# Operands of matrix products moved to addresses that are multiples of 512 bytes, in a four-layer trunk on one Trainium2 core

## The chip, the cores and the metric

The kernel runs on one core of one Trainium2 chip. The metric is the device time of one execution in microseconds (us). A core has a matrix engine (TensorE, called PE in the profile, with its weight loads shown apart as PEld), a vector engine (VectorE, DVE), an activation engine (ScalarE, ACT), GpSimd (POOL), and queues that start transfers (SP, ACT and POOL). Its working memory has 128 partitions; an address here is a byte offset inside a partition, and all 128 partitions use the same one.

## The reference

The model takes 512 tokens of 1,024 features through four sublayers, each added to the residual stream after a root-mean-square norm: multi-head latent attention (MLA), a feed-forward layer (MLP), gated linear attention (GLA), and a second MLP; a last norm follows.

```python
for i in range(DEPTH):                    # DEPTH = 2
    xn = rms_norm(x, norm_mix[i])
    mix = mla_mixer(xn, ...) if i % 2 == 0 else gla_mixer(xn, ...)
    x = x + mix
    x = x + jnp.square(jax.nn.relu(rms_norm(x, norm_mlp[i]) @ w_up[i])) @ w_down[i]
return rms_norm(x, final_norm)
```

MLA has 8 heads, projections of low rank for queries (384) and for keys and values (256), a rotary key and a causal softmax over 512 keys. GLA has 4 heads with a decay per key feature, accumulated over the sequence. The MLPs go from 1,024 to 4,096 features and back.

## The kernel before

Everything is float32. A product is made of three passes on the matrix engine: each operand is split into a high part (the rounded copy, type fp32r) and a low part (the rest), and high x high, high x low and low x high are summed (`mm3`, lines 109 to 114). In a pass the *stationary* operand, 128 columns (512 bytes of a partition), is loaded into the array, and the *moving* operand, up to 512 columns (2,048 bytes), streams past it. A pass on a type other than fp32r is issued twice by the compiler, except transposes (`tr`, line 129), which multiply by the tile `ident`.

Weights come from memory into the tiles `wraw` and `comb`, are split by ACT (line 104) and DVE (line 107) into `wh` and `wl`, and are used at once. Activations live in tiles called `set`, 2,048 or 4,096 bytes each. Each MLP works by blocks of 512 hidden features with a seven-product scheme on quarters of the matrices: `up_product` (line 939) has moving operands of 256 columns, which are either parts of the `set` tiles ("11", "21", "22") or of four combined tiles `T1` to `T4` (the profile calls them `T`, since it leaves numbers out); `down_product` (line 948) has moving operands of 512 columns out of `wh` and `wl` and stationary ones out of `set`.

The order of the instructions on each engine comes from a scheduler and a few explicit rules of order in the kernel. Tiles are placed by pools: `const` and `sb` live to the end, `rk` (`rope_keep`), `keep` and `pp` (attention), `ap` (`mla_attn`), `fast` (MLP) and `gp` (GLA) live for a stage and share the room above. A pool's tiles follow each other, each rounded up to 32 bytes; small tiles between large ones shift all that follow. A tile with one value or a few per partition (`stat`, `srstd`, `cols`, `gms`, `D`, `rtok`) costs 32 bytes.

In the built program before, 265 tiles `wh`, 265 `wl` and all 158 `set` tiles begin 32 bytes past a multiple of 512; `T1` to `T4` and `comb` 320 past; the latent tiles of attention `cq..` 128 past, and `ckv..`, `kh`, `kl`, `qh`, `ql`, `KA`, `KB`, `PTh` and `PTl` 192 past; GLA's `ADh` and `qd` 320 past, its `kth`, `ktl` and `S` 384 past; `ident` 128 past.

Of the passes on fp32r, by columns of the moving operand and by whether both operands stand at the same offset past a multiple of 512 (counted in the built program):

| columns | same offset before | other offsets before | same offset after | other offsets after |
|---|---|---|---|---|
| 512 | 2,744 | 212 | 2,934 | 22 |
| 384 | 24 | 40 | 64 | 0 |
| 256 | 1,032 | 1,504 (of these `T`: 1,344) | 2,536 | 0 |
| 128 | 0 | 16 | 16 | 0 |

Of the kernel before, what the change touches and what calls it, by code (L numbers as in the profile page):

```python
# [18 lines left out]
P = 128  # L19
D = 1024  # L20
# [30 lines left out]
def trunk_kernel(ctx: ExitStack, tc: tile.TileContext, t_in: dict, out: bass.AP):  # L51
# [71 lines left out]
            return ACT.activation(*a, **k)  # L123

    ident = const.tile([P, P], F32, name="ident")
    make_identity(nc, ident)

    def tr(psum, src):
# [18 lines left out]
    rope_es = ExitStack()  # L147
    rk = rope_es.enter_context(tc.tile_pool(name="rope_keep", bufs=1, reuse_waits="tile"))

    gains = const.tile([P, N_GAIN + NT + 32], F32, name="gains")  # L150
    pos_i = gains[:, N_GAIN : N_GAIN + NT].bitcast(I32)
    invf = gains[:, N_GAIN + NT :]

# [5 lines left out]
    def load_x(q, j):  # L159
        q.dma_start(xall[:, j], x_in[:, j])  # L160

    eps_t = const.tile([P, 1], F32, name="eps_t")
    DVE.memset(eps_t, EPS)
    one_t = const.tile([P, 1], F32, name="one_t")
    DVE.memset(one_t, 1.0)
    ones_r = const.tile([P, P], F32R, name="ones128")
    ones128 = f(ones_r)
    DVE.memset(ones128, 1.0)
    ident_b = rk.tile([P, P], BF16, name="ident_b")
# [2 lines left out]
    DVE.memset(causal, 0.0)  # L172
    POOL.affine_select(causal, causal, [[-1, P]], ALU.is_ge, NEG, base=0, channel_multiplier=1)

    def inv_tile(n, pool):
        t = pool.tile([P, P], F32R, name=f"inv{n}")
        DVE.memset(f(t), 1.0 / n)
        return t

    inv_dr = inv_tile(D, const)  # L180
    inv_d = f(inv_dr)

    RB = 32
    row_eps = rk.tile([3 * RB, 1], F32, name="row_eps")
    row_mix = rk.tile([3 * RB, 1], F32, name="row_mix")
    for r, (e, m) in enumerate(((EPS * EPS, EPS), (Q_PART * EPS * EPS, Q_PART * EPS), (EPS, 1.0))):
        DVE.memset(row_eps[r * RB : (r + 1) * RB], e)
        DVE.memset(row_mix[r * RB : (r + 1) * RB], m)  # L190
# [82 lines left out]
    def small_rstd(ms, n, scale):  # L273
        l = sm(n)
        act_e(l, ms, AF.Ln, bias=eps_t, scale=scale)
        y0 = sm(n)
        act_e(y0, l, AF.Exp, scale=-0.5)
        e = sm(n)
        DVE.tensor_scalar(e, ms, scale, EPS, ALU.mult, ALU.add)
        a = sm(n)  # L280
        DVE.tensor_tensor(a, e, y0, ALU.mult)
        b = sm(n)
        DVE.scalar_tensor_tensor(b, a, -0.5, y0, ALU.mult, ALU.mult)
        r = sb.tile([P, n], F32, tag="srstd", bufs=4, name=uname("srstd"))
        DVE.scalar_tensor_tensor(r, b, 1.5, y0, ALU.add, ALU.mult)
        return r

# [5 lines left out]
    def rope_turns():  # L293
        sh = (P, NT, 32)
        es = ExitStack()
        rp = es.enter_context(tc.tile_pool(name="rope", bufs=1, reuse_waits="tile"))

        def tmp(shape, dt=F32):
            return rp.tile(list(shape), dt, tag="rope", bufs=8, name=uname("rope"))

        pos = tmp((P, NT))
        POOL.tensor_copy(pos, pos_i)
        ang, part = tmp(sh), tmp(sh)
        POOL.tensor_tensor(
            ang, pos.unsqueeze(2).to_broadcast([P, NT, 32]), invf.unsqueeze(1).to_broadcast([P, NT, 32]), ALU.mult
        )
        ah = tmp(sh, F32R)
        POOL.tensor_copy(ah, ang)
        al = tmp(sh)
        POOL.tensor_tensor(al, ang, f(ah), ALU.subtract)  # L310
        frac = Fraction("0.15915494309189533576888376337251436203445964574046")
        c = []
        for _ in range(4):
            e = 0
            while frac * 2**e < 2048:
                e += 1
            c.append(Fraction(int(frac * 2**e), 2**e))
            frac -= c[-1]
        c = [float(v) for v in c]

        def wrap(t):
            m = part
            POOL.tensor_scalar(m, t, 1.0, MAGIC, ALU.mult, ALU.add)
            POOL.tensor_scalar(m, m, 1.0, -MAGIC, ALU.mult, ALU.add)
            POOL.tensor_tensor(t, t, m, ALU.subtract)

        acc = tmp(sh)
        POOL.tensor_scalar(acc, f(ah), c[0], 0.0, ALU.mult, ALU.add)
        wrap(acc)
        wrap(acc)  # L330
        for src, n, wraps in ((f(ah), 1, 1), (al, 0, 1), (f(ah), 2, 1), (al, 1, 1), (f(ah), 3, 0), (al, 2, 0), (al, 3, 0)):
            t = tmp(sh)
            POOL.tensor_scalar(t, src, c[n], 0.0, ALU.mult, ALU.add)
            for _ in range(wraps):
                wrap(t)
            POOL.tensor_tensor(acc, acc, t, ALU.add)
        r = rk.tile([P, 2, NT, 32], F32, name="rope_turns")
        for n, shift in enumerate((0.25, 0.0)):
            t = tmp(sh)
            POOL.tensor_scalar(t, acc, 1.0, shift, ALU.mult, ALU.add)  # L340
            wrap(t)
            POOL.tensor_scalar(r[:, n], t, 0.4999999, -0.4999999, ALU.min, ALU.max)
        es.close()
        return r
# [29 lines left out]
    def mla(layer, nrm, first, pools):  # L374
# [111 lines left out]
        for t in range(NT):  # L486
            tk = slice(t * P, (t + 1) * P)
            for hf in range(2):
                p = bank("bc"[hf])
                for k in range(2):  # L490
                    mm3(p, cut(CVL[k], slice(None), tk), cut(wv[k], slice(None), 0, slice(hf * 512, hf * 512 + 512)), k == 0, k == 1)
                if (t, hf) == (1, 1):
                    pr = bank("c")
                    for i in range(NT):
                        tr(pr[:, i * 3 * RB : (i + 1) * 3 * RB], rows[:, i * P : (i + 1) * P])
                    cols = keep.tile([P, NT, 3], F32, tag="cols", name="cols")
                    DVE.tensor_copy(cols, pr[:, : NT * 3 * RB].rearrange("p (t a r) -> p t a r", t=NT, a=3)[:, :, :, 0])
                    VP.append((1, 1, p))
                    for i in (1, 0, 3, 2):
                        evac_v(*VP[i])  # L500
                elif t < 2:
                    VP.append((t, hf, p))
                else:
                    evac_v(t, hf, p)
            if t == 1:
                r_kv = sb.tile([P, S], F32, tag="rstd", bufs=2, name=uname("rstd"))
                for i in range(P // RB):
                    SP.dma_start(r_kv[i * RB : (i + 1) * RB], rows[:RB])
                for j in range(2):
                    y = tmp()  # L510
                    DVE.scalar_tensor_tensor(y, pkv[j], gcol("kvn", 2 * layer + j), r_kv, ALU.mult, ALU.mult)
                    hi, lo = (keep.tile([P, S], F32R, tag=f"ckv{j}{x}", name=f"ckv{j}{x}") for x in "hl")
                    split(y, hi, lo)
                    CKV.append((hi, lo))
# [140 lines left out]
        def scores(h, q, k):  # L655
# [3 lines left out]
            for i in (0, 2, 1, 3):  # L659
# [9 lines left out]
                    PE.matmul(o, q[1][:, qk], k[0][:, :n], start=False, stop=False)  # L669
                PE.matmul(o, QST[h][:, tk], KA[:, :n], start=False, stop=False)  # L670
                PE.matmul(o, QST[h][:, tk], KB[:, :n], start=False, stop=True)  # L671
            stats = [sb.tile([P, 4], F32, tag="stat", bufs=8, name=uname("stat")) for _ in range(NT)]


            def mask(o, m):
# [521 lines left out]
    def gla(layer, nrm, vtag, ytag):  # L1197
# [82 lines left out]

        own = tmp((P, NT, P))
        DVE.tensor_tensor(own, nrm.rstd.rearrange("p (t c) -> p t c", t=NT), ident.unsqueeze(1).to_broadcast([P, NT, P]), ALU.mult)
        rtok = sb.tile([P, NT], F32, tag="rtok", name="rtok")
        DVE.reduce_sum(rtok, own, AX.X)


# [76 lines left out]
        def levels(h):  # L1363
# [28 lines left out]
            def pairs():  # L1392
                grow(1)
                later = qd.rearrange("p (t n a) -> p t n a", t=NT, a=2)[:, :, :, 1]
                ACT.activation(q[:, :, P:], later, AF.Copy)

                def evacuate(p, a):
                    DVE.copy_predicated(a, ident_i.unsqueeze(1).to_broadcast([P, 2, P]), p[:, :, :P])
                    odd = a.rearrange("p t (n b) -> p t n b", b=2)[:, :, :, 1]
                    DVE.copy_predicated(odd, mask_1.unsqueeze(1).to_broadcast([P, 2, 64]), p[:, :, P:])  # L1400

                return lambda: two_tiles(k, q, evacuate)
# [49 lines left out]


            def turned():
                at["D"] = gp.tile([P, NT], F32, tag="D", bufs=2, name=uname("D"))
                DVE.tensor_copy(at["D"], T[P])
                e = gp.tile([P, 2 * S], F32R, tag="T", bufs=3, name=uname("qd"))
                at["q"] = e[:, : S - P], e[:, S : 2 * S - P]
                split(qd[:, P:], *at["q"])

                def products():
                    p = bank("c")[:, : S - P]
                    for i in range(NT - 1):
                        tr(p[:, i * P : (i + 1) * P], k[:, i * P : (i + 1) * P])
                    at["k"] = tuple(gp.tile([P, S - P], F32R, tag=x, bufs=2, name=uname(x)) for x in ("kth", "ktl"))
                    split(p, *at["k"])

                return products
# [59 lines left out]

        def gated(h):
            at, hf = AT[h], h // 2  # L1530
            at["ms"] = sb.tile([P, NT], F32, tag="gms", bufs=2, name=uname("gms"))
            for i in range(NT):
                if i % 2:
                    for r in (i - 1, i):
# [131 lines left out]
    rope_es.close()  # L1666
    n_mlp0 = Norm(ND, inv_dr, "mlp", 0)
    out_proj(t_in["mla_w_o"][0], O, n_mlp0, begun)
    ident_i = const.tile([P, P], I32, name="ident_i")
    DVE.tensor_copy(ident_i, ident)  # L1670

    def block_mask(name, m, blocks, group):
        n = P // group
# [70 lines left out]
```

## Time and profile before

| | |
|---|---|
| times of 3 runs | 1057.3, 1057.37, 1059.06 us; median 1057.37 |
| the profiled execution | 1057.37 us, of which the span from first to last instruction is 1055.6 |
| PE busy | 1045.5 us (99% of the span), 5,966 passes |
| DVE / ACT / POOL busy | 876.0 / 698.6 / 113.4 us |
| transfers | 149.97 MB, mean 142 GB/s |
| granted PE clock | 0.999 |

A pass begins while the one before is still draining, so the duration of one pass (some 390 ns for 512 columns) is longer than the distance from one start to the next. What a stage costs is that distance. It is read from the timeline, which merges equal neighbours into a row with the start of the first, or from the chain of work, which gives the length of a stretch and how many passes it has.

### The profile page before, as it was taken

The numbers are of one execution on the slowest core, as the hardware profiler recorded it, in microseconds if no ns is written. First come the engines' busy times: TensorE is split into PE (matmuls) and PEld (weight loads), VectorE is DVE, ScalarE is ACT, GpSimd is POOL, SyncE is SP. The second block draws the span as 40 slices with busy tenths as digits, with TensorE's granted clock in tenths as the row PEclk, the third lists the DMA queues.
The fourth block names the chain that finished last, engine by engine and source line by source line (L and its number), as shares of the span: only waits on it lengthen the run. The fifth ranks groups of instructions, "written<-read, shape, count | busy, mean of one in ns | idle before, by whom it ended". The sixth has DMA issues, their size and how long they took to land.

```text
span 1055.6 us, 15598 instructions
## 1 busy us (share of the span) xinstructions
PE 1045.5 (99%) x5966; PEld 913.7 (87%) x5966; DVE 876.0 (83%) x1340; ACT 698.6 (66%) x1074; POOL 113.4 (11%) x128
## 2 busy tenths in 40 slices
PE   9999999999999999999999999999999999999997
PEld 7888888889999999998888888878889999999985
DVE  7899977979889889898686498469889989989993
ACT  7667664577777767766445565655667777777784
POOL 7410011201101111000000000000011010010000
PEclk9999999999999999999999999999999999999999
DMA  7311235866966976842322221444496696696622
GB/s 231 90 51 41 81 79 160 238 176 150 235 181 150 229 192 146 221 147 93 90 80 80 80 80 51 126 105 132 110 248 132 178 254 140 176 249 152 165 81 80
DMA packets 120493, 149.97 MB, mean 142 GB/s; under 512 B 9345, under 2 KB 86145, under 8 KB 120289
## 3 DMA queue, kind: packets, MB, share of 16 engines
q1 hardware_dynamic: 95920, 117.76, 34.4%
q0 software_dynamic: 22400, 29.36, 17.4%
q10 hardware_dynamic: 2096, 1.84, 0.6%
q8 instruction: 47, 0.77, 0.3%
q14 instruction: 30, 0.24, 0.1%
HBM read 144.49 MB, written 4.19 MB: 141 GB/s over the span
## 4 chain that ended last, share of the span: by engine, by line
PE 95%; ACT 2%; DVE 2%; issue 0%; DMA 0%; ACTq 0%; SPq 0%; DVEq 0%
PE ps L939 26%; PE ps L948 25%; PE ps L112 10%; PE ps L114 10%; PE ps L113 10%; PE ps L1133 2%; PE ps L1388 2%; PE ps L129 1%; PE ps L1168 1%; PE ps L408 1%; PE ps L1515 1%; DVE wl L107 0%; PE ps L671 0%; PE ps L1438 0%; PE ps L667 0%
## 5 line engine op out<-in xcount | busy, mean ns | idle before, releaser
L948 PE MATMUL ps<-wh,set 128*128 128x512 f32 x784 | 258.5, 390 | 0.0
L107 DVE TENSOR_TENSOR wl<-wraw,wh 128x1024 fp32r<-128x1024 f32 x139 | 169.4, 1221 | 39.7 <-ACT wh L104 39.4
L104 ACT ACTIVATE wh<-wraw 128x1024 fp32r<-128x1024 f32 x139 | 145.9, 1053 | 82.1 <-PE ps L113 38.3
L948 PEld LDWEIGHTS ps<-wh,set 128*128 128x128 f32 x784 | 147.3, 188 | 28.8
L104 ACT ACTIVATE wh<-comb 128x1024 fp32r<-128x1024 f32 x112 | 118.8, 1061 | 62.8 <-PE ps L939 41.9
L939 PE MATMUL ps<-T,wh 128*128 128x256 f32 x896 | 159.8, 279 | 0.0
L948 PE MATMUL ps<-wl,set 128*128 128x512 f32 x392 | 153.7, 392 | 0.0
L107 DVE TENSOR_TENSOR wl<-comb,wh 128x1024 fp32r<-128x1024 f32 x112 | 136.7, 1220 | 18.6 <-ACT wh L104 16.9
L939 PEld LDWEIGHTS ps<-T,wh 128*128 128x128 f32 x896 | 140.5, 188 | 4.5
L939 PE MATMUL ps<-T,wl 128*128 128x256 f32 x448 | 125.1, 279 | 1.0 <-DVE wl L107 1.0
L939 PE MATMUL ps<-set,wh 128*128 128x256 f32 x672 | 122.6, 283 | 0.0
L939 PEld LDWEIGHTS ps<-set,wh 128*128 128x128 f32 x672 | 107.4, 191 | 3.2
L112 PE MATMUL ps<-set,wh 128*128 128x512 f32 x280 | 109.3, 392 | 0.7 <-ACT set L1557 0.3
L113 PE MATMUL ps<-set,wh 128*128 128x512 f32 x280 | 109.4, 391 | 0.0
L114 PE MATMUL ps<-set,wl 128*128 128x512 f32 x280 | 109.0, 390 | 0.0
L939 PE MATMUL ps<-set,wl 128*128 128x256 f32 x336 | 95.2, 283 | 0.0
L939 PEld LDWEIGHTS ps<-T,wl 128*128 128x128 f32 x448 | 84.2, 188 | 1.5 <-DVE wl L107 1.4
L948 PEld LDWEIGHTS ps<-wl,set 128*128 128x128 f32 x392 | 73.8, 188 | 11.6
L928 POOL DMA_DIRECT2D comb<-in_mlp_w_down_dram x28 | 33.6, 1201 | 421.0 <-DMA comb<-in_mlp_w_down_dram 155.5
L939 PEld LDWEIGHTS ps<-set,wl 128*128 128x128 f32 x336 | 64.3, 191 | 0.0
L112 PEld LDWEIGHTS ps<-set,wh 128*128 128x128 f32 x280 | 52.5, 188 | 12.6 <-ACT wh L104 1.0
L114 PEld LDWEIGHTS ps<-set,wl 128*128 128x128 f32 x280 | 52.6, 188 | 11.2 <-DVE wl L107 0.4
(396 smaller groups left out, 2024.2 us busy)
## 6 DMA issues: line engine op xcount, KB each, us to landing
comb<-in_mlp_w_down_dram SPq DMA_DIRECT2D x74, 512.0 KB, 5.0
wraw<-in_mlp_w_up_dram SPq DMA_DIRECT2D x32, 1024.0 KB, 5.8
comb<-in_mlp_w_down_dram POOLq DMA_DIRECT2D x28, 512.0 KB, 7.7
wraw<-in_gla_w_in_dram SPq DMA_DIRECT2D x12, 1024.0 KB, 5.3
comb<-in_mlp_w_up_dram SPq DMA_DIRECT2D x14, 512.0 KB, 3.8
comb<-in_mlp_w_up_dram POOLq DMA_DIRECT2D x14, 512.0 KB, 8.4
wraw<-in_mlp_w_up_dram POOLq DMA_DIRECT2D x14, 512.0 KB, 7.2
wraw<-in_mla_w_o_dram SPq DMA_DIRECT2D x4, 1024.0 KB, 5.0
```

The source lines that it names most:

```text
L104: order(ACT.activation(hi, src, AF.Copy))
L107: lo_eng.tensor_tensor(lo, src, f(hi), ALU.subtract)
L112: PE.matmul(psum, wh, xh, start=start, stop=False)
L113: PE.matmul(psum, wh, xl, start=False, stop=False)
L114: PE.matmul(psum, wl, xh, start=False, stop=stop)
L129: PE.transpose(psum, src, ident[: src.shape[0], : src.shape[0]])
L408: PE.matmul(p, w[:, i, j * P : (j + 1) * P], x, start=start, stop=stop)
L928: POOL.dma_start(t, q(b, *more), accum_op=ALU.add)
L939: PE.matmul(o, a_, x_, start=start and j == 0 and k == 0 and n == 0, stop=k == KH - 1 and n == 2, skip_group_check=True)
L948: PE.matmul(o, x_, w_, start=start and k == 0 and n == 0, stop=k == 1 and n == 2, skip_group_check=True)
L1133: PE.matmul(p, a, x, start=False, stop=k == 3 and n == 2, skip_group_check=True)
L1388: PE.matmul(p[:, t - t0], k[:, t * P : (t + 1) * P], moving[:, t], start=True, stop=True)
```

## The change

It moves addresses. Small tiles of `sb`, `rk`, `keep` and `gp` (`srstd`, `stat`, `cols`, `gms`, `D`, `row_eps`, `row_mix`) go into `const`, the tiles `ones128` and `inv1024` stand earlier in it, and `gains`, `rtok` and `rope_turns` are given more room than they use, so that every later pool begins at a multiple of 512. The int32 copy of the identity (`ident_i`) is dropped; the masked copies of GLA take the bits of `ident` itself. After it all moving operands of passes on fp32r begin at multiples of 512, and all stationary ones but those of 22 small passes (the gate's projection of 96 columns and the means of the first norms); `ident` stays 128 past one.

```diff
     ident = const.tile([P, P], F32, name="ident")
+    ones_r = const.tile([P, P], F32R, name="ones128")
+    inv_dr = const.tile([P, P], F32R, name=f"inv{D}")
+    eps_t = const.tile([P, 1], F32, name="eps_t")
+    one_t = const.tile([P, 1], F32, name="one_t")
+    row_eps = const.tile([96, 1], F32, name="row_eps")
+    row_mix = const.tile([96, 1], F32, name="row_mix")
...
-    gains = const.tile([P, N_GAIN + NT + 32], F32, name="gains")
+    gains_room = const.tile([P, 176], F32, name="gains")
+    gains = gains_room[:, : N_GAIN + NT + 32]
...
-        r = sb.tile([P, n], F32, tag="srstd", bufs=4, name=uname("srstd"))
+        r = const.tile([P, n], F32, tag="srstd", bufs=4, name=uname("srstd"))
...
-        r = rk.tile([P, 2, NT, 32], F32, name="rope_turns")
+        r = rk.tile([P, 2, NT, 56], F32, name="rope_turns")[:, :, :, :32]
...
-                    cols = keep.tile([P, NT, 3], F32, tag="cols", name="cols")
+                    cols = const.tile([P, NT, 3], F32, tag="cols", name="cols")
...
-            stats = [sb.tile([P, 4], F32, tag="stat", bufs=8, name=uname("stat")) for _ in range(NT)]
+            stats = [const.tile([P, 4], F32, tag="stat", bufs=8, name=uname("stat")) for _ in range(NT)]
...
-        rtok = sb.tile([P, NT], F32, tag="rtok", name="rtok")
+        rtok = sb.tile([P, 48], F32, tag="rtok", name="rtok")[:, :NT]
...
-                    DVE.copy_predicated(a, ident_i.unsqueeze(1).to_broadcast([P, 2, P]), p[:, :, :P])
+                    DVE.copy_predicated(a, ident.bitcast(I32).unsqueeze(1).to_broadcast([P, 2, P]), p[:, :, :P])
...
-                at["D"] = gp.tile([P, NT], F32, tag="D", bufs=2, name=uname("D"))
+                at["D"] = const.tile([P, NT], F32, tag="D", bufs=2, name=uname("D"))
...
-            at["ms"] = sb.tile([P, NT], F32, tag="gms", bufs=2, name=uname("gms"))
+            at["ms"] = const.tile([P, NT], F32, tag="gms", bufs=2, name=uname("gms"))
...
-    ident_i = const.tile([P, P], I32, name="ident_i")
-    DVE.tensor_copy(ident_i, ident)
```

Leaving line numbers and buffer numbers aside, the rows of PE, ACT and SP are the same in both programs, in the same order and with the same waits. On POOL the two writes of `rope_turns` become strided (128x4x32 in place of 128x128). On DVE one row goes, near the start. Before:

```order
27 L107 TENSOR_TENSOR wl_164<-wraw_ckv,wh_163 128x512
28 L1670 COPY ident_i<-ident 128x128
29 L250 TENSOR_SCALAR set_167<-xT,gains,set_167 128x512
30 L250 TENSOR_SCALAR set_170<-xT,gains,set_170 128x512
31 L107 TENSOR_TENSOR wl_299<-wraw_296,wh_298 128x1024
```

and the same place after:

```order
27 L107 TENSOR_TENSOR wl_164<-wraw_ckv,wh_163 128x512
28 L247 TENSOR_SCALAR set_167<-xT,gains,set_167 128x512
29 L247 TENSOR_SCALAR set_170<-xT,gains,set_170 128x512
30 L107 TENSOR_TENSOR wl_299<-wraw_296,wh_298 128x1024
31 L107 TENSOR_TENSOR wl_304<-wraw_296,wh_303 128x1024
```

The copy at row 28 is gone and its neighbours have closed up; nothing else stands elsewhere.

More of the change, by code (lines that the diff above doesn't have):

```diff
@@ L160, in load_x @@
         q.dma_start(xall[:, j], x_in[:, j])
-    eps_t = const.tile([P, 1], F32, name="eps_t")
     DVE.memset(eps_t, EPS)
-    one_t = const.tile([P, 1], F32, name="one_t")
     DVE.memset(one_t, 1.0)
-    ones_r = const.tile([P, P], F32R, name="ones128")
     ones128 = f(ones_r)
@@ L173, in trunk_kernel @@
     POOL.affine_select(causal, causal, [[-1, P]], ALU.is_ge, NEG, base=0, channel_multiplier=1)
[L175 to L180, printed above, removed]
+    DVE.memset(f(inv_dr), 1.0 / D)
     inv_d = f(inv_dr)
     RB = 32
-    row_eps = rk.tile([3 * RB, 1], F32, name="row_eps")
-    row_mix = rk.tile([3 * RB, 1], F32, name="row_mix")
     for r, (e, m) in enumerate(((EPS * EPS, EPS), (Q_PART * EPS * EPS, Q_PART * EPS), (EPS, 1.0))):
```

## Prediction

> **What bounds the kernel now.** First the page.
>
> ```profile
> span 1055.6 us, 15598 instructions
> PE 1045.5 (99%) x5966; PEld 913.7 (87%) x5966; DVE 876.0 (83%) x1340; ACT 698.6 (66%) x1074; POOL 113.4 (11%) x128
> PE 95%; ACT 2%; DVE 2%; issue 0%; DMA 0%; ACTq 0%; SPq 0%; DVEq 0%
> L948 PE MATMUL ps<-wh,set 128*128 128x512 f32 x784 | 258.5, 390 | 0.0
> L939 PE MATMUL ps<-T,wh 128*128 128x256 f32 x896 | 159.8, 279 | 0.0
> L939 PE MATMUL ps<-T,wl 128*128 128x256 f32 x448 | 125.1, 279 | 1.0 <-DVE wl L107 1.0
> L939 PE MATMUL ps<-set,wh 128*128 128x256 f32 x672 | 122.6, 283 | 0.0
> ```
>
> PE is busy 99% of the span and is 95% of the chain that ended last. Who made PE wait is told by the list of waits, here the whole of PE's:
>
> ```profile
> PE ps L1652 <- DVE ones L168: 1.2, 1, 1.2
> PE ps L939 <- DVE wl L107: 1.0, 2, 0.5
> PE ps L408 <- ACT set L249: 0.4, 1, 0.4
> PE ps L112 <- ACT set L1557: 0.3, 1, 0.3
> PE ps L664 <- ACT pr L123: 0.2, 1, 0.2
> PE ps L112 <- DVE xT L784: 0.2, 1, 0.2
> ```
>
> They sum to 3.3 us. So hardly anyone feeds PE too late, and the time is the number of passes by the distance between their starts. This change leaves their order, so only the distance can move it. In the groups above the `T` passes of `up_product` last 279 ns and the `set` passes of the same line 283; columns, weights' tiles and stage are the same, only the moving tile differs. The chain of work has whole stretches (start, length, passes), the first two of L939 with `T` and with `set`:
>
> ```profile
> 357.22 2.80 PE ps L939 x24
> 362.76 2.87 PE ps L939 x24
> 494.33 10.89 PE ps L1133 x48
> ```
>
> 24 passes in 2.80 us are 116.7 ns each; 24 in 2.87 are 119.6, and in this one the first pass, after another shape, is shorter. The timeline gives it without that, from the third to the last of a stretch of `set` and of one of `T`, 21 distances each:
>
> ```profile
> 362.83 0.28 PE L939 MATMUL ps<-set,wl 128*128 128x256 f32 x1
> ...
> 365.36 0.28 PE L939 MATMUL ps<-set,wl 128*128 128x256 f32 x1
> 365.48 0.40 PE L948 MATMUL ps<-wh,set 128*128 128x512 f32 x1
> ...
> 367.09 0.39 PE L948 MATMUL ps<-wl,set 128*128 128x512 f32 x1
> ...
> 368.22 0.40 PE L939 MATMUL ps<-set,wh 128*128 128x256 f32 x2
> ...
> 374.08 0.28 PE L939 MATMUL ps<-T,wl 128*128 128x256 f32 x1
> ...
> 376.53 0.28 PE L939 MATMUL ps<-T,wl 128*128 128x256 f32 x1
> ```
>
> `set`: 2.53/21 = 120.5 ns; `T`: 2.45/21 = 116.7. With 119.6 as the other end I take 120.0 for `set`; `T` is faster by 3.3 ns (2.9 to 3.8). Passes of 512 columns run at 10.89/48 = 226.9 ns in the last stretch of the fence before. In a block of the MLP (365.48 to 368.22) 12 take 2.74 us, 228.3 each: the first seven 230 (1.61 us to 367.09), the last five 226 (1.13 us). They settle.
>
> From 226.9 and 120.0 a column costs (226.9 - 120.0)/256 = 0.418 ns. So 256 columns are 106.9 and 512 are 213.8, and each pass has a rest: 13.1 ns for `set` and for 512 columns, 9.8 for `T`. Transposes show a smaller one:
>
> ```profile
> 479.75 1.47 PE L1126 MATMUL ps<-ident,xT 128*128 128x128 f32 x12
> L1126 PE MATMUL ps<-ident,xT x12: 272/272/273, 479.8 to 481.0; 128*128 128x128 f32 x12
> ```
>
> Eleven distances take 1.47 - 0.27 = 1.20 us, 109 ns; at two steps a column 128 columns are 106.9, which leaves 2 ns. The passes on fp32r therefore lose some 8 to 11 ns each on something, and what differs between `T` and `set` is the address. In the program before, `set` and its stationary partner both begin 32 bytes past a multiple of 512; `T` begins 320 past, its partner 32.
>
> Do unequal offsets help, then? Two other stages say what they do. In attention 36 passes of 512 columns have a moving operand at 32 and a stationary one at 128 (`cq`); from their third to their 34th start are 31 distances. In GLA nine passes of 256 columns have `S` at 384 and `qd` at 320, both multiples of 64:
>
> ```profile
> 50.71 0.39 PE L114 MATMUL ps<-wh,cq0l 128*128 128x512 f32 x1
> ...
> 57.97 0.40 PE L112 MATMUL ps<-set,cq2h 128*128 128x512 f32 x1
> 602.44 1.23 PE L1515 MATMUL ps<-S,qd 128*128 128x256 f32 x9
> 603.50 0.39 PE L112 MATMUL ps<-set,wh 128*128 128x512 f32 x1
> ```
>
> The first run at 7.26/31 = 234.2 ns and don't settle, 7.3 above the equal ones; the second at 1.06/9 = 117.8, between `T` and `set`. In this trace equal offsets are the best for 512 columns and the worst for 256.
>
> **The change, part by part.** What it does to the time hangs on one question: is it the difference of the two offsets that counts, or where each stands? After it nearly all pairs are equal, as `set` with `wh` is now, but at 0 in place of 32. I take the difference, because stretches of hundreds of passes with equal offsets all behave alike here, and the one row where both offsets are multiples of 64 (117.8) is no faster than `T`. Then:
>
> - `T` joins `set`: 896 + 448 = 1,344 passes by +3.3 ns = +4.5 us (3.9 to 5.1). All on the path, since PE waits for nobody.
> - 160 passes of 256 columns in GLA and attention go from 117.8 to 120.0: +0.35 (0 to 0.5).
> - 212 passes of 512 columns have unequal offsets. The 36 fall from 234.2 to 226.9: -0.26. The other 176, in attention, stand in short groups between other shapes, where 512 columns need seven passes to settle: at most -7.3 x 176 = -1.3, half of it taken. Together -0.9 (-0.3 to -1.5).
> - The 2,744 passes of 512 columns with equal offsets, and 1,032 of 256: nothing.
> - The copy on DVE goes:
>
> ```profile
> L1670 DVE CAST ident_i<-ident x1: 314/314/314, 13.2 to 13.2; 128x128 int32<-128x128 f32 x1
> L342 POOL TENSOR_SCALAR rope_turns<-rope x2: 744/1023/1302, 34.5 to 37.8; 128x128 f32<-128x128 f32 x2
> L348 ACT ACTIVATE rope_tabs<-rope_turns x1: 421/421/421, 53.3 to 53.3; 128x256 f32<-128x256 f32 x1
> ```
>
> At 13.2 us PE has work queued, so its 0.31 us are worth nothing, or -0.3 at the most. The strided write on POOL ends near 39 us and is read at 53.3, so it could take five times as long. Transfers and DVE and ACT operations get new addresses too; PE's list of waits names no transfer, and its waits for DVE and ACT are 3.3 us in all, so I set this at nothing, with -3 as the most that faster feeders could bring; what slower ones could cost is bounded by no row, but DVE and ACT are idle 17% and 34% of the span.
>
> Sum: +4.5 + 0.35 - 0.9 = +3.9 us on the profiled execution's 1057.37 (1055.6 of span and 1.8 around it), which is also the median of the runs: 1061.3, with 2.4 to 5.3 by the bounds, 1059.8 to 1062.7.
>
> **The rivals.** *No effect of addresses, or one that cancels* (about 1057.4): the moving and the stationary operand are read without touching each other, and the 3.3 ns of `T` come from something else; or passes of 256 columns come to 117.8 everywhere (1,344 by +1.1, 1,032 by -2.2, -0.8 net) beside -0.9 in attention: 1055.7. Against the first speaks that `T` and `set` alternate on one line all through both MLPs and differ each time. The Trainium skill stands on its side: "SBUF — State Buffer" (Specifications, and Who interferes with whom) has lines of 16 bytes, which every tile here already respects, two separate read ports for PE, and a PE that never waits on anyone. By it the change would be worth 0; this trace, with 120.0 against 116.7, does not agree.
>
> *The place counts, and a round one is better* (faster). `T`, whose moving operand begins at a multiple of 64, has 3.3 ns less rest than `set`; if the stationary side brings as much again, all rests fall to 6.5 ns: 226.9 to 220.3 for 2,744 passes (-18.1), 234.2 to 220.3 for 212 (-2.9), 120.0 to 113.4 for 1,032 (-6.8), -3.3 for `T` (-4.4), 117.8 to 113.4 for 160 (-0.7): -32.9, 1024.5. The ends: only `set` comes down to `T` (-3.4) and attention gains 0.9, 1053.1; or every rest falls to the 2 ns of the transposes, 215.9 and 109.0: 2,744 by 12.4 from the MLP's 228.3, 212 by 18.3, 1,032 by 11.0, 1,344 by 7.7, 160 by 8.8, -61 together, 996. For it: a rest of 10 to 13 ns stands where transposes have 2, and of all pairs no fp32r pass begins at a multiple of 512 today, so that the trace cannot rule it out. Against: `S` with `qd` at 117.8, where both are multiples of 64, so that it would need rounder places than 64. The Trainium skill, "TensorE: Matmul & The Clock Gate" (Back-to-back issue gap), has an isolated gap of N/2.4 + 2.5 ns, which would be 216 and 109 here, near that last end; no fp32r row of this trace comes to it.
>
> *Settling is lost* (slower by much). The 512-column passes settle at 226.9 only at offset 32 with 32; no stretch in this trace has them both at a rounder place for long. If at 0 with 0 they stay where the 36 of attention are, 234.2: +5.9 on the 228.3 of the MLP for 2,744 passes is +16.2, with -0.8 for the 256: 1072.8. It decides where the last stretch of L1133 takes 11.2 us and not 10.9.
>
> That the change does not do what it says is ruled out: the built program has the addresses.
>
> **How the numbers follow.** 0.2% is 2.1 us here, about what a measurement of this kernel can tell. Forecast 0.37; a round place is better 0.36; settling lost 0.14; no effect or cancelled 0.13. Faster 0.36, same 0.13, slower 0.37 + 0.14 = 0.51. The likeliest is 1061.3, its own range 1059.8 to 1062.7. The range goes down to the middle price of the faster case, 1024 (about half of that case lies above it), and up to 1073: 0.37 + 0.13 + 0.2 + 0.1 = 0.8.
>
> **What would show it.** Right: stretches of 24 passes of L939 that all take 2.87 us, none 2.80; the 36 of attention in 8.2 us in place of 8.4; L1133 still 10.9 for 48. Wrong: `T` at 2.80 or less with `set` also below 2.87 (the place counts), L1133 well under 10.9 (a round place is better) or near 11.2 (settling is lost), or nothing changed in any of these.

## Result and the profile after

The changed kernel takes 1061.05 us (median of 8 runs, 1060.75 to 1061.46) where the kernel before takes 1057.47 (8 runs, 1057.3 to 1059.06): 1.0032 times as long, 95% interval 1.0021 to 1.0043. Slower by 3.6 us; the prediction was 1061.3.

From the page of the changed kernel: span, engines, the chain by engine, and the four groups that answer to those shown of before (line 936 is 939 before, 945 is 948).

```profile
span 1059.4 us, 15597 instructions
PE 1049.3 (99%) x5966; PEld 918.3 (87%) x5966; DVE 876.1 (83%) x1339; ACT 698.4 (66%) x1074; POOL 113.3 (11%) x128
PE 96%; DVE 2%; ACT 2%; issue 0%; DMA 0%; ACTq 0%; SPq 0%; DVEq 0%
L945 PE MATMUL ps<-wh,set 128*128 128x512 f32 x784 | 258.7, 391 | 0.0
L936 PE MATMUL ps<-T,wh 128*128 128x256 f32 x896 | 163.5, 283 | 0.0
L936 PE MATMUL ps<-set,wh 128*128 128x256 f32 x672 | 122.6, 283 | 0.0
L936 PE MATMUL ps<-T,wl 128*128 128x256 f32 x448 | 127.0, 283 | 1.0 <-DVE wl L107 1.0
```

The span grew by 3.8 us and PE's busy time by the same 3.8, while DVE and ACT did not move. The `T` groups now last 283 ns, as `set` does; they lasted 279. The wide group and the `set` group stand as they were, within a nanosecond.

The four longest of PE's six rows of waits in the changed kernel (us in total, times, longest). All six are those of before but for L661, with one wait of 0.2 us more:

```profile
PE ps L1649 <- DVE ones L172: 1.2, 1, 1.2
PE ps L936 <- DVE wl L107: 1.0, 2, 0.5
PE ps L405 <- ACT set L246: 0.4, 1, 0.4
PE ps L661 <- ACT pr L123: 0.4, 2, 0.2
```

The chain of work of the changed kernel: two stretches of 24 narrow passes, the first with `T` and the second with `set`, and the last wide stretch.

```profile
357.85 2.87 PE ps L936 x24
363.47 2.87 PE ps L936 x24
495.92 10.89 PE ps L1130 x48
```

The chain of before has 54 stretches of 24 at 2.80 us and 39 at 2.87; that of the changed kernel has 93 at 2.87 and none at 2.80. The stretch of 48 wide passes has not moved: 10.89 before and after.

The timeline of the changed kernel at the two places in attention and GLA:

```profile
50.67 0.40 PE L114 MATMUL ps<-wh,cq0l 128*128 128x512 f32 x1
...
57.74 0.39 PE L112 MATMUL ps<-set,cq2h 128*128 128x512 f32 x1
604.14 1.24 PE L1512 MATMUL ps<-S,qd 128*128 128x256 f32 x9
605.22 0.40 PE L112 MATMUL ps<-set,wh 128*128 128x512 f32 x1
```

From the third to the 34th of the 36 passes, 31 distances take 7.07 us, 228.1 ns each (234.2 before). The nine passes of `S` take 1.08 us, 120.0 each (117.8 before). Both now have equal offsets, and both moved to the price of equal offsets: down for 512 columns, up for 256.

Added up from the starts of the passes in the two traces, pass by pass:

| passes | before, us | after, us | change | predicted |
|---|---|---|---|---|
| 1,344 of 256 columns, `T` | 158.53 | 162.38 | +3.85 | +4.5 |
| 160 of 256 columns, unequal before | 19.16 | 19.46 | +0.29 | +0.35 |
| 212 of 512 columns, unequal before | 51.24 | 50.68 | -0.57 | -0.9 |
| 2,744 of 512 and 1,032 of 256, equal before | 757.97 | 758.10 | +0.13 | 0 |
| all the rest | | | +0.1 | 0 |
| together | | | +3.8 | +3.9 |

### The profile page after: what moved, and what is told of

Same layout as the page of the kernel before. It is cut to its first block, busy times and chain, and to the rows that moved or that the text cites. A ratio compares the mean times of both kernels' runs of the same rounds, so it can differ in the third digit from the quotient of the medians.

```text
span 1059.4 us, 15597 instructions
## 1 busy us (share of the span) xinstructions
PE 1049.3 (99%) x5966; PEld 918.3 (87%) x5966; DVE 876.1 (83%) x1339; ACT 698.4 (66%) x1074; POOL 113.3 (11%) x128
## 4 chain that ended last, share of the span: by engine, by line
PE 96%; DVE 2%; ACT 2%; issue 0%; DMA 0%; ACTq 0%; SPq 0%; DVEq 0%
PE ps L936 26%; PE ps L945 25%; PE ps L112 11%; PE ps L114 11%; PE ps L113 10%; PE ps L1130 2%; PE ps L1385 2%; PE ps L135 1%; PE ps L1165 1%; PE ps L405 1%; PE ps L1512 1%; DVE wl L107 0%; PE ps L668 0%; PE ps L1435 0%; PE ps L664 0%
## 5 line engine op out<-in xcount | busy, mean ns | idle before, releaser
L936 PE MATMUL ps<-T,wh 128*128 128x256 f32 x896 | 163.5, 283 | 0.0
L104 ACT ACTIVATE wh<-comb 128x1024 fp32r<-128x1024 f32 x112 | 118.7, 1060 | 67.4 <-PE ps L936 43.7
L936 PEld LDWEIGHTS ps<-T,wh 128*128 128x128 f32 x896 | 143.3, 191 | 4.5
L936 PEld LDWEIGHTS ps<-set,wl 128*128 128x128 f32 x336 | 64.3, 191 | 0.0
L104 ACT ACTIVATE set<-set 128x512 fp32r<-128x512 f32 (+1 forms) x70 | 41.9, 603 | 31.4 <-PE ps L945 29.4
```

Source lines behind the costliest of these rows:

```text
L104: order(ACT.activation(hi, src, AF.Copy))
L936: PE.matmul(o, a_, x_, start=start and j == 0 and k == 0 and n == 0, stop=k == KH - 1 and n == 2, skip_group_check=True)
```

## Experiments

Theory 1 is the prediction's: the spacing of passes hangs on the difference between the two operands' offsets, not on where they stand. The rivals are that the place of the moving operand counts, that other engines' accesses do it, or that another part of the change carries the cost. Times of before are those of the same sets of runs, 1057.1 to 1057.3 us.

**Places and differences on an idle core (`m_places`).** A kernel of its own, run once, of which this is the core; `m` and `s` are in bytes:

```python
def stretch(n, m, s, times=30):
    for i in range(times):
        mv = MV[:, m // 4 + (i % 2) * S : m // 4 + (i % 2) * S + n]
        st = ST[:, s // 4 + (i % 8) * P : s // 4 + (i % 8) * P + P]
        PE.matmul(o[:, :n], st, mv, start=i == 0, stop=i == times - 1)
```

> This kernel computes none of the model: on an otherwise idle core it runs stretches of 30 fp32r passes, each stretch with the moving operand m bytes and the stationary one s bytes past a multiple of 512, for 33 pairs (m, s), 512 and 256 columns, the whole list twice, the second time backwards. Theory 1 (the difference of the two counts): every pair with m = s settles at 226.7 ns (512 columns) and 120.0 (256), whatever the place; pairs with m unlike s take about 117 for 256 columns and about 234 for 512. Theory 2 (the place of the moving operand counts): the pairs with m = 320 are fast for 256 columns whatever s, and (0, 32) is like (0, 0). Theory 3 (the two reads don't touch each other, and the spacing of the kernel comes from other engines' accesses): with the core idle all pairs take the same, below 120 and below 226.7.

Its page (PE and DVE) and its timeline in six windows (start, length, passes of 256 columns) show it. The pairs (m, s) of the six rows are, in order, (0, 0), (32, 0), (64, 0), (256, 0), (32, 32) and (320, 32):

```profile
span 712.4 us, 8104 instructions
PE 708.3 (99%) x4020; PEld 618.6 (87%) x4020; DVE 2.0 (0%) x2; POOL 0.2 (0%) x4
249.78 2.69 PE L73 MATMUL ps<-mv,st 128*128 128x256 f32 x21
256.56 2.95 PE L73 MATMUL ps<-mv,st 128*128 128x256 f32 x24
260.03 3.02 PE L73 MATMUL ps<-mv,st 128*128 128x256 f32 x25
281.38 2.44 PE L73 MATMUL ps<-mv,st 128*128 128x256 f32 x19
327.31 2.67 PE L73 MATMUL ps<-mv,st 128*128 128x256 f32 x21
344.99 2.96 PE L73 MATMUL ps<-mv,st 128*128 128x256 f32 x24
```

With 0.28 us taken off for the last pass, the first row has 20 distances in 2.41 us, 120.5 ns; the second 23 in 2.67, 116; the third 24 in 2.74, 114; the fourth and fifth 120; the last 116.5. Settled, from the starts of the single passes (pairs at multiples of 32; a range, where pairs or rounds differ):

| m - s, modulo 256 | 512 columns, ns | 256 columns, ns |
|---|---|---|
| 0: (0,0) (32,32) (64,64) (128,128) (192,192) (256,256) (256,0) (0,256) | 226.7 | 120.0 |
| 32: (32,0) (288,0) (320,32) | 233.2 to 233.4 | 116.6; once 117.8 |
| 64: (64,0) (320,0) (384,320) | 228.9 | 113.3 or 117.8 |
| 96: (96,0) (352,0) (128,32) | 233.3 to 233.6 | 120.1 to 120.2 |
| 128: (128,0) (384,0) (0,128) | 232.4 to 233.5 | 118.6 to 118.8 |
| 160: (160,0) (416,0) (192,32) (32,128) | 234.3 | 117.3 to 118.8; once 120.0 |
| 192: (192,0) (448,0) (0,64) | 233.3 to 233.5 | 113.3 or 117.8 |
| 224: (224,0) (480,0) (0,32) (32,320) | 233.2 to 233.4 | 118.3 to 118.5 |

Theory 1 holds in what it says of equal pairs: six places give one price. The difference counts modulo 256, not 512, and with a sign (64 and 192 are unlike at 512 columns). The two prices that it gave for unequal pairs, about 117 and 234, were too simple: they spread from 113.3 to 120.2 and from 228.9 to 234.3, a difference of 96 is no faster than 0 at 256 columns, and at 64, 160 and 192 one difference shows more than one spacing. The third theory falls: with DVE and ACT idle the spacings are those of the kernel.

**T alone moved apart again (`t_apart`).** In the changed kernel, one line that moves `T` and `comb`; PE doesn't read `comb`:

```diff
         fast = es.enter_context(tc.tile_pool(name=f"fast{layer}", ...
+        fast.tile([P, 72], F32, name=f"room{layer}")
```

> The changed kernel with T1 to T4 and comb alone moved 288 bytes on, so that moving and stationary operand of the T passes differ by 288 again, as before the change, all else as after it. Theory 1 (difference): the T passes fall back to 116.7 ns, 1,344 x 3.3 = 4.5 us, and the gain of attention stays: about 1056.7, just under the kernel before. Theory 2 (place, 320 past): 288 is another place than 320; if only 320 is fast, no change, 1061.1. Theory 3 (other causes in the change): T stays at 120.0, 1061.1.

Measured 1057.39 us against 1057.13 of before, ratio 1.0001 (0.9992 to 1.0009): the loss is gone. From the chain, a stretch with `T`, and from the groups, `T` and `set`:

```profile
335.12 2.80 PE ps L937 x24
L937 PE MATMUL ps<-T,wh 128*128 128x256 f32 x896 | 159.9, 279 | 0.0
L937 PE MATMUL ps<-set,wh 128*128 128x256 f32 x672 | 122.6, 283 | 0.0
```

All 54 stretches of `T` are back at 2.80 us. The expected step below the kernel before did not show: attention's gain is 0.3 us net, too small to measure.

**T alone made equal (`t_level`).** The same line with 56 in place of 72, in the kernel before: `T` goes from 320 to 32, all else stays.

> The kernel before with T1 to T4 and comb alone moved 224 bytes on, from 320 to 32 past a multiple of 512, equal to their stationary partner; all else as before. Theory 1: the T passes go to 120.0 ns, +4.5 us: about 1061.9, slower than the changed kernel by what that gains in attention. Theory 3 (other parts of the change carry its cost): 1057.4.

Measured 1061.62 us against 1057.13, ratio 1.0042 (1.0028 to 1.0055). The span and the same rows:

```profile
span 1059.3 us, 15598 instructions
335.53 2.87 PE ps L940 x24
L940 PE MATMUL ps<-T,wh 128*128 128x256 f32 x896 | 163.5, 283 | 0.0
```

Moving `T` (and `comb`) alone costs 4.5 us (3.0 to 5.8 by the interval), about what the whole change costs (2.2 to 4.5), with the copy on DVE and the small tiles as they were. Together the two runs show which part of the change is the loss: the one that makes `T` and its partner equal.

**Other widths (`m_columns`).** As the first kernel, over widths, run once:

> Like the run of single places, none of the model is computed: stretches of 24 passes for 7 widths (128 to 512 columns) at differences of 0, 32, 64, 128, 160 and 192 bytes, then a few small differences (4, 8, 48, 72, 80 bytes), then stationary operands that change place from pass to pass. Theory 1: at difference 0 the spacing of every width settles on a multiple of 16 cycles of 2.4 GHz (6.67 ns), as 288 cycles for 256 columns and 544 for 512 do; with 64 it is shorter for narrow passes. Rival: the equal pair is slow at 256 columns by chance of that width, and other widths show no pattern.

At difference 0 the spacings are 120.0, 146.7, 173.3 and 226.7 ns for 256, 320, 384 and 512 columns: 18, 22, 26 and 34 times 6.67 ns, the time of 16 columns. 448 columns gave 202.7 and no such multiple, and 128 and 192 columns take 111.7 ns, both the same, with no pattern in the difference. So the first half of the expectation holds from 256 columns on, with that one exception. The second does not: at 64 only 256 columns (117.8 here) and 448 (200.0) are shorter; 128, 192, 320 and 384 stay. The rival is not ruled out: 320 columns take 146.7 at all six differences, 384 and 512 are never faster apart than equal, and 256 is the one width that is faster apart at most differences.

Of the small differences, 4 bytes gave 123.3 ns at 256 columns and 236.7 at 512, more than equal offsets at both; 8 gave 126.7 in one round and 116.7 in the other at 256; 48, 72 and 80 gave 118.3 to 121.3. So to be apart is not enough to be faster at 256 columns: it matters by how much. In the last part the stationary operand alternates between 0 and 64: 116.7 ns at 256 columns and 230.0 at 512; which of two neighbouring weight loads counts can't be told from it.

**T at the difference that was best on the idle core (`t_64`).** 16 in place of 72:

> The changed kernel with T1 to T4 and comb alone moved 64 bytes on. Theory 1 in its sharper form (the difference modulo 256 sets the spacing, 64 is the best for 256 columns): T passes of 113.3 ns in place of 120.0, 56 stretches of 24 with the first pass left out, 1,288 x 6.67 = 8.6 us: about 1052.5. If the T passes fall into the other spacing that the idle core showed for differences of 64 (117.8): 2.9 us less, about 1058. Theory 2 (only the idle core shows it; here DMA and the other engines disturb it): about 1057, as at a difference of 288.

Measured 1059.37 us, ratio to before 1.0021 (1.0011 to 1.0030): a miss. The second figure of the expectation, about 1058, has the narrow passes right but nothing for the wide ones. The chain and the group:

```profile
335.17 2.83 PE ps L937 x24
L937 PE MATMUL ps<-T,wh 128*128 128x256 f32 x896 | 161.2, 280 | 0.0
```

In every one of the 54 stretches the passes took the slower of the two spacings seen at this difference, 117.8 ns. Beside that, the 12 wide passes behind each stretch took 2,757 ns in place of 2,748: their own addresses had not changed, so their time depends on what ran ahead of them. Per block of 24 + 12 that is 33 ns less than at equal offsets, 1.8 us in 54 blocks, and 1061.05 - 1.8 = 1059.3 is what was measured.

**set and T at 64, wide products mostly equal (`a_64`).** 64 bytes between `wl` and the first `set_A`, 192 behind the last, and the 64 ahead of `T`:

```diff
+        if not roomy:
+            roomy.append(sb.tile([P, 16], F32, name="room"))
...
+        if len(roomy) == 1:
+            roomy.append(sb.tile([P, 48], F32, name="room2"))
...
+        fast.tile([P, 16], F32, name=f"room{layer}")
```

> The changed kernel with T1 to T4, comb and the eight tiles set_A (the normalised activations, moving operand of all 256-column passes of the MLPs) 64 bytes further on than their partners modulo 256. Theory 1: T -8.6, the 1,008 set passes -6.4; the 520 passes of 512 columns with set_A moving go to 228.9, +1.1, the 384 with set_A stationary to 233.4, +2.5: in all -11.4, about 1049.7. At 117.8 for the narrow passes: about 1059.

Measured 1060.60 us, ratio 1.0031 (1.0019 to 1.0042). All 93 narrow stretches have the same length:

```profile
335.42 2.83 PE ps L943 x24
L943 PE MATMUL ps<-set,wh 128*128 128x256 f32 x672 | 120.8, 280 | 0.0
```

The narrow passes fell into 117.8 again, `set` as `T` (-4.0 us together against the changed kernel), and the wide passes with unequal partners gave it back (+3.9 with all the rest).

**Everything but the weights at 64 (`all_64`).** Only the first of the three edits above:

> The changed kernel with everything above the weights' tiles wh and wl moved 64 bytes on, activations and T alike. Theory 1, with the sign of the difference counting for 512 columns as on the idle core: narrow passes -15.0; 1,000 passes of 512 columns with the activation moving (difference 64) go to 228.9, +2.1; 1,608 with the weights moving (difference -64) to 233.4, +6.2 in the MLPs and +2.5 elsewhere: about 1056.8, 7 us slower than the kernel that moves only set_A and T. Rival (equality alone matters, no sign): 1,000 and 1,608 alike, about 1051.

Measured 1065.43 us, ratio 1.0077 (1.0064 to 1.0090). Against the changed kernel the narrow passes gain 4.3 us (15.0 expected) and the rest loses 9.2 (10.8 expected). The chain's last stretch has the activation moving, so +64, and the group of `down_product` the weights moving, so -64:

```profile
497.97 11.00 PE ps L1134 x48
L949 PE MATMUL ps<-wh,set 128*128 128x512 f32 x784 | 261.9, 394 | 0.0
```

The first is 229.2 ns a pass (228.9 on the idle core); in `down_product` the 12 wide passes of a block take 2,800 ns, 233.3 each. The wide passes' price and its sign carry over to the kernel, against the rival without a sign; only the narrow ones' better spacing does not.

**Four differences at once (`t_mix`).** Before each of the four tiles a piece of room of its own:

```diff
+        fast.tile([P, 48], F32, name=f"room{layer}")
...
+                if name != "T2":
+                    fast.tile([P, {"T3": 24, "T1": 32, "T4": 8}[name]], F32, name=f"room{name}{layer}")
```

> The changed kernel with T1 to T4 at four different distances from their partner, modulo 256: T1 160, T2 192, T3 32, T4 192 (as 448), everything else as after the change. On the idle core 32 gave 116.7 ns, 160 gave 117.3 to 118.6, 192 either 113.3 or 117.8, according to how a stretch began. Theory 1 (the difference sets the spacing in the kernel too, and the passes ahead of a stretch decide between two spacings): T3 116.7, T1 117.3 to 118.6, T2 and T4 alike, both 113.3 or both 117.8. If 113.3, moving all of T to 192 would make the kernel some 4 us faster than before the change. Rival (a place matters as well as a difference): T2 and T4, whose places differ by 256, come out unlike.

One run, 1057.25 us (the kernel before in the same set: 1057.27). From the chain, a stretch each of `T2`, `T1`, `T3` and `T4`, by their order in the kernel:

```profile
256.15 2.83 PE ps L939 x24
261.69 2.85 PE ps L939 x24
272.89 2.80 PE ps L939 x24
278.44 2.83 PE ps L939 x24
```

By the starts of the passes the settled spacings are 116.7 ns (`T3`, 32), 118.7 (`T1`, 160) and 117.7 (`T4`, 192). `T2`, 192 as well, is 117.7 in 12 of its 14 blocks. The other two are the first of each MLP, where PE waits in the midst of `T2`; this is the first of them:

```profile
214.32 0.38 PE L939 MATMUL ps<-T,wl 128*128 128x256 f32 x1 [0.50 <-DVE wl L107]
214.78 0.28 PE L939 MATMUL ps<-T,wl 128*128 128x256 f32 x1
...
216.14 0.28 PE L939 MATMUL ps<-T,wl 128*128 128x256 f32 x1
```

From the second row to the third are 12 distances, 1.36 us, 113.3 ns each. So `T2` and `T4` are alike in the other 12 blocks, as theory 1 has it and against the rival, and the fast spacing does come up in the kernel: with the same tile and difference, where PE had just waited. What counts is the block with the wide passes behind:

| difference of the narrow passes | 24 narrow, ns | 12 wide behind, ns | together, ns |
|---|---|---|---|
| 0 (`T` and `set`) | 2,872 | 2,748 | 5,620 |
| 64 | 2,830 | 2,757 | 5,587 |
| 160 | 2,854 | 2,726 | 5,580 |
| 192 | 2,826 | 2,720 | 5,546 |
| 32 | 2,803 | 2,744 | 5,547 |

All sums are multiples of 6.67 ns, within the trace's nanosecond. 32, the difference of 288 that the kernel before has, is as good as any that was tried.

**Narrow passes unequal, wide ones equal (`w_apart`).** The experiments point to a version that takes the better price for both. The weights of `up_product` alone are written 224 bytes into larger tiles (the lines that make room for them are left out here):

```diff
-    def piece(raw, a, n, order=lambda i: i):
-        hi = sb.tile([P, a, n], F32R, tag="wh", bufs=3, name=uname("wh"))
-        lo = sb.tile([P, a, n], F32R, tag="wl", bufs=3, name=uname("wl"))
+    def piece(raw, a, n, order=lambda i: i, at=0):
+        rooms = [sb.tile([P, 2 * S + 64], F32R, tag=t, bufs=3, name=uname(t)) for t in ("wh", "wl")]
+        hi, lo = (t[:, at : at + a * n].rearrange("p (a n) -> p a n", a=a) for t in rooms)
...
-            w = piece(a, KH, 256)
+            w = piece(a, KH, 256, at=56)
```

> The changed kernel in which every tile wh and wl gets 256 bytes more, and the weights of up_product alone are written 224 bytes into them; room for that comes from small tiles (the warm-up products take inv1024 in place of ones128, eps_t and one_t share a tile, gains and rtok lose their padding). All 2,352 passes of 256 columns in the MLPs then have a difference of 32 modulo 256, all passes of 512 columns keep 0. Theory 1: a stretch of 24 narrow passes with the 12 wide ones behind it took 5,620 ns at difference 0 and 5,547 at 32 in every run so far; 54 such blocks with T and 39 with set gain 73 ns each, 6.8 us: about 1054.3, some 3 us under the kernel before. Rival (T is special, say because its tiles lie in another part of the memory than set): only T gains, about 1057.2.

Measured 1054.78 us (1054.36 to 1056.86), ratio to before 0.9978 (0.9969 to 0.9987). The page's first rows, a stretch of the chain, and the groups of `T` and `set`:

```profile
span 1052.7 us, 15596 instructions
PE 1042.3 (99%) x5966; PEld 910.5 (86%) x5966; DVE 875.5 (83%) x1338; ACT 699.4 (66%) x1074; POOL 113.1 (11%) x128
333.76 2.80 PE ps L935 x24
L935 PE MATMUL ps<-T,wh 128*128 128x256 f32 x896 | 159.7, 279 | 0.0
L935 PE MATMUL ps<-set,wh 128*128 128x256 f32 x672 | 119.7, 280 | 0.0
```

`set` now runs as `T` does, so `T` was never special, and this kernel beats both others: 6.3 us under the changed one (6.8 expected), 2.6 under the one before. A block takes 5,553 ns, one step of 6.67 more than the 5,547 expected; 93 such steps are 0.6 us, about what is missing.

## Why the prediction was right

*What bounds it.* PE's busy time and the span both moved by 3.8 us, and PE's waits by 0.2 at most: the distance between passes was the whole of it, as the prediction took it to be.

*`T` joins `set`.* +3.85 us where +4.5 (3.9 to 5.1) stood: right in sign and cause, just under its range in size. The step that was mis-sized is the 3.3 ns per pass: this is the settled distance, and it was put on all 1,344. A whole stretch of 24 differs by 2.87 - 2.80 = 0.07 us, 2.9 ns a pass, since its first distance goes the other way: behind the wide passes it is 113.3 ns at equal offsets and was 119.1 for `T` before. 54 stretches by 70 ns are the 3.8. The row for it was in the prediction, and gave its lower bound.

*160 narrow passes, 212 wide ones.* +0.29 and -0.57, inside their ranges of 0 to 0.5 and -0.3 to -1.5. The 36 passes fell from 8.5 to 8.3 us, by 0.2 as forecast; the other 176 brought 0.36 us of the 1.3 at most, where half was taken.

*What was luck.* The cost of `T` was put 0.65 us too high and the saving of the wide passes 0.33 too high, and these offset each other in part: the sum, +3.9 against +3.8, is nearer than its terms. The forecast itself stood at 0.37 beside 0.36 for a faster kernel, and its full range, 1024 to 1073, held a gain as well: the sign was far from settled by the prediction's own chances, and the experiments settled it.

*Copy and strided write.* No cost and no gain shows. In the changed kernel the strided write runs from 34.7 to 38.5 us and is read at 53.3:

```profile
L339 POOL TENSOR_SCALAR rope_turns<-rope x2: 750/948/1146, 34.7 to 37.7; 128x128 f32<-128x128 f32 x2
L345 ACT ACTIVATE rope_tabs<-rope_turns x1: 419/419/419, 53.3 to 53.3; 128x256 f32<-128x256 f32 x1
```

*The rivals.* No effect: excluded by `t_level`. A round place is better: a pair at (0, 0) costs 120.0 and 226.7, as at (32, 32), and so at every place tried; the row that spoke for it, `T` at a rounder place with less rest, was the difference all along. Settling is lost: it was not, the last stretch of L1130 takes 10.89 us as before. The row that spoke against the round place, `S` with `qd` at 117.8, was weaker than the prediction took it for: it is a pair 64 bytes apart, and other pairs 64 apart ran at 113.3 on the idle core, faster than `T`. That it pointed the right way was partly luck. The Trainium skill's "SBUF — State Buffer" (Who interferes with whom), by which the two reads of PE go through ports of their own, would have made all pairs alike; the idle core does not agree, with 120.0 ns for every equal pair and 116.6 to 117.8 for pairs 32 apart.

*What stays open.* That the two operands' addresses act together on the spacing is shown; by what path is not. Why a stretch at difference 64 or 192 settles at 113.3 ns in one case and 117.8 in another is shown only as far as that it depends on what ran ahead of it. Why equal offsets are slow at 256 columns and not at 320, 384 or 512 is open too.

## What to carry to other kernels

Read the distance between starts, not the duration, and compare groups that differ in one operand alone: a difference of 3 ns a pass was worth 4 us here. Aligning every operand to the same round address is not neutral for fp32r products on a kernel bound by PE: in this kernel the passes of 512 columns were best at equal offsets modulo 256, and the passes of 256 columns 32 bytes apart (on the idle core, 4 and 96 bytes apart were no better than equal). That step from all equal to the better of the two was worth 6.3 us of 1061. Try a spacing that a separate measurement promises inside the kernel before counting on it, since it can depend on the passes ahead.

## What was not expected of the hardware

- The period of the difference is 256 bytes: (256, 0) costs what (0, 0) does, 120.0 and 226.7 ns, and (320, 0) at 512 columns what (64, 0) does, 228.9.
- For 512 columns the sign counts: a moving operand 64 bytes further on than the stationary one takes 228.9 ns, one 64 bytes less far 233.4.
- Blocks come in whole steps of 6.67 ns, the time of 16 columns, though the spacings of single widths need not (448 columns take 202.7): the blocks of 24 + 12 passes took 5,620, 5,587, 5,580, 5,553 and 5,547 ns, which are 843, 838, 837, 833 and 832 steps.
- Passes of 128 and of 192 columns take the same 111.7 ns one after another, at each of the six differences tried.
- None of this needs other engines: a core on which PE alone works shows the same spacings as the kernel does (226.7 and 120.0 ns at equal offsets, 116.6 at 32 apart).
